# A merge that alternates computed and loaded gates, two attention blocks turned ahead, and pools of slots opened anew for each stage

## The chip, the cores and the metric

One core of one Trainium2 chip. The metric is device time in microseconds (us) of one execution of the whole program; the engines are TensorE (PE in the profile, its weight loads PEld), VectorE (DVE), ScalarE (ACT), GpSimd (POOL) and SyncE (SP), beside 16 DMA engines. SP and ACT issue the DMAs, each into its own queue.

## The reference

Two layers over 1024 latent tokens and 256 context tokens (1280 in all, 10 tiles of 128) of width 1024. Layer 1 needs no context output, so it has 8 tiles of queries where layer 0 has 10.

```python
p = modulated(x) @ w_in                      # all branches, their SiLU gates, 4 x 1024 merge gates
u0, u1, u2, u3 = neighbourhood, latent, RG-LRU, grouped-query branch of p   # each [tokens, 256]
m = sum(sigmoid(gate_i) * (u_i @ w_branch[i]) for i in range(4))            # [tokens, 1024]
x = layer_norm(alpha * x + g * (m @ w_out))  # g from the modulation vector
```

All matmuls that matter are taken in three products of a number split in a high and a low part (hi·hi, lo·hi, hi·lo), so each logical product of 128 rows is three matmul instructions.

## The kernel before, in words

The program text is written in stages, and a scheduler orders the instructions of each engine from it; each engine then works through its own list in order. Storage comes from pools: `sl` gives slots of [128, 1280] floats (13 of them, for K and V, softmax rows, accumulators, branch inputs, output rows), `wp` gives pairs of split weights `whi`/`wlo` of 512 columns (10 of them, with 2 raw buffers `wraw`), `tp` the short-lived tiles (`tmp`, `ph`, `pl`, `q`), and PSUM gives two banks each for `mm` and `t` and a wide one. A tile that takes a buffer waits for the last use of the tile that had it. Both pools live for the whole program.

One layer (function `layer`) runs so:

- `g_proj`, then `m_proj` and `a_proj` woven with the LRU branch. `put_t` (line 320 on) turns projected rows, splits them into `ph`/`pl` tiles and stores them to DRAM from ACT's queue; K, V and q are loaded from there later. The first loads of attention (K, V and q of the first head, `first_loads`) stand between `m_proj` and `a_proj`.
- Attention: 12 heads (4 grouped-query, 4 latent, 4 neighbourhood), each in units of 2 or 3 query tiles: 2, 3, 3, 2 in layer 0 and 3, 3, 2 in layer 1. `attend` makes the scores of one unit; `values` turns softmax blocks (transposes on PE, a split into `ph`/`pl` by ACT and DVE) and multiplies them with V, and is pumped between later scores. It turns one block ahead of the one it multiplies. SP loads q for the next unit (`fetch`, into a ring of three q tiles) and, at the first unit of a head, K and V of the next head (`ahead_kv`). Each q comes as two halves, and the second half of the one under way stands behind K and V in SP's queue.
- Beside attention `gates()` computes merge gates (24 matmuls for 128 output columns and 512 tokens) and stores them: all eight chunks c of the last two branches in `M_ORDER` = (2, 3, 1, 0).
- `merge()` goes over branches 2, 3, 1. Branches 2 and 3 compute their gates (24 matmuls and 6 for the branch, per chunk and group of tokens), branch 1 loads them (6 matmuls); the sigmoid is ACT's, the product DVE's, the addition to `acc` POOL's for loaded gates and else DVE's.
- `last` (line 1005 on) does branch 0 with loaded gates, splits each finished `acc` into `xh`/`xl` (40 pieces over both layers), and loads w_out.
- `outp` (line 1039 on) multiplies with w_out tile by tile, adds the residual, normalises, and in layer 0 stores `x1` and turns the result back for layer 1.

Of the kernel before, what the change touches and what calls it, by code (L numbers as in the profile page):

```python
# [16 lines left out]
D = 1024  # L17
# [19 lines left out]
G_PRE = 2  # L37
W_A = 30
W_B = 26
UNITS = [(2, 3), (5, 3), (8, 2)]  # L40
NBIAS = (E_N + M_N) * 64
# [5 lines left out]
def hybrid_kernel(ctx: ExitStack, tc, a):  # L47
# [8 lines left out]
    sm = ctx.enter_context(tc.tile_pool(name="sm", bufs=6))  # L56
    lc = ctx.enter_context(tc.tile_pool(name="lc", bufs=2))
    dr = ctx.enter_context(tc.tile_pool(name="dr", bufs=2, space=DRAM))
    ps_mm = ctx.enter_context(tc.tile_pool(name="ps_mm", bufs=2, space=PSUM))
# [57 lines left out]
    def spare():  # L117

        turns[0] += 1
        tag = ("tmp", "ph", "tmp", "pl", "tmp", "ph", "pl")[turns[0] % 7]  # L120
        return tp.tile([128, 512], F32, tag=tag, name=nm("spare"), bufs=3 if tag == "tmp" else 2)
# [5 lines left out]
    def slot(dt=F32, w=NT, s="sl"):  # L127
        return sl.tile([128, w], dt, tag="sl", name=nm(s))
# [65 lines left out]
    def row_stats(src):  # L194
        st = sm.tile([128, 2, 6], F32, tag="bnst", name=nm("bnst"))
# [36 lines left out]
    def split_w(raw, shape):  # L232
# [3 lines left out]
        hi = wp.tile([128, 512], F32R, tag="whi", name=nm("whi"))  # L236
        lo = wp.tile([128, 512], F32R, tag="wlo", name=nm("wlo"))
# [7 lines left out]
    def load_w(src, shape):  # L245
        n = 1
        for d in shape[1:]:
            n *= d
        raw = wp.tile([128, 512], F32, tag="wraw", name=nm("wraw"), bufs=2)
# [4 lines left out]
        return split_w(raw, shape)  # L254
# [37 lines left out]
    def layer(l, xh, xl, need_ctx, gate, finish, side, side2, ahead=None):  # L292
# [24 lines left out]
        gate_d = {i: dram([KC, 128, NT], F32, f"gates{i}") for i in M_ORDER[4 - G_PRE:]}  # L317
        u_d = [dram([2, 128, NT], F32, f"u{i}") for i in range(4)]

        def put_t(dst, t, first, src, rows=128):  # L320
# [6 lines left out]
            hi = tp.tile([128, 4, 128], F32R, tag="ph", name=nm("th"), bufs=2)  # L327
# [8 lines left out]
        def put_v(dst, t, src3):  # L336

            n = src3.shape[1]
            vt = tp.tile([128, 4, 128], F32R, tag="ph", name=nm("vt"), bufs=2)
# [112 lines left out]
        def lru_steps():  # L452
# [24 lines left out]
            for c in range(2):  # L477
# [20 lines left out]
                raw = wp.tile([128, 512], F32, tag="wraw", name=nm("wraw"), bufs=2)  # L498
# [67 lines left out]
        def attend(h, unit, qs, y, rcp, scores, vt):  # L566
# [7 lines left out]
            queue.append([values(64 * (h % 2), y, qts, blocks, pts, vt), len(blocks) + 1])  # L574

        def values(o, y, qts, blocks, pts, vt):
# [5 lines left out]
            def turn(vb, q0, cols):  # L582
# [4 lines left out]
                ph = tp.tile([128, 512], F32R, tag="ph", name=nm("ph"), bufs=2)  # L587
# [8 lines left out]
            st = None  # L596
            for i, b in enumerate(blocks):
                nx = turn(*b)
# [5 lines left out]
            product(nb - 1, *st)  # L604
# [83 lines left out]
        def m_load():  # L688
# [14 lines left out]
            for src, n in ((a["mla_w_uq"][l, 0:128], 384), (a["mla_w_uq"][l, 128:256], 384), (a["mla_w_ukv"][l], 512)):  # L703
                raw = wp.tile([128, 512], F32, tag="wraw", name=nm("wraw"), bufs=2)
# [11 lines left out]
        def m_steps():  # L716
# [25 lines left out]
            def second(t, has_q, y, kr):  # L742
# [4 lines left out]
                ch = tp.tile([128, 512], F32R, tag="ph", name=nm("ch"), bufs=2)  # L747
# [138 lines left out]
        def attention(jobs):  # L886
# [37 lines left out]
        def gates():  # L924

            for i in M_ORDER[4 - G_PRE:]:
                for c in range(KC):
                    w = load_chunk(w_in, C_GATE + i * D + c * 128)
                    for g in qgroups:
                        gs = slice(g[0], g[0] + g[1])  # L930
                        ps = mm()
                        xs = xs_g(g)
                        for k in range(0, KC, 2):
                            mm_b(ps[:, :g[1]], w[k:k + 2], lambda j: xs(k + j), k == 0, k == KC - 2)
                            if k < KC - 2:
                                yield
                        s = tmp()
                        act.copy(s[:, :g[1]], ps[:, :g[1]])
                        act.dma_start(gate_d[i][c, :, gs], s[:, :g[1]])
                        yield  # L940

        jobs = [make(h) for make in (g_job, m_job, a_job) for h in range(4)]
        att = attention(jobs)
        run(f"g_proj{l}", g_steps())

        def first_loads():
            next(att)
            yield

        weave(("", chain((f"m_proj{l}", m_steps()), (f"g_att{l}", first_loads()), (f"a_proj{l}", a_steps())), W_A),  # L950
              (f"lru{l}", lru_steps(), W_B))
        ticks = sum(len(qts) + len(blocks) for job in jobs for qts, blocks in job[3])
        fill.update(gen=gates(), rate=4 * KC * G_PRE * len(qgroups) / ticks, due=0.0)
# [22 lines left out]
        def merge():  # L976
            for bi, i in enumerate(M_ORDER[:3]):
                uh, ul = load_u(i)
                for c in range(KC):
                    w = None if i in gate_d else load_chunk(w_in, C_GATE + i * D + c * 128)  # L980
# [3 lines left out]
                    for g in qgroups:  # L984
                        gs = slice(g[0], g[0] + g[1])
                        sgm = tmp()
                        if w is None:
                            pm = sgm
                            sp.dma_start(sgm[:, :g[1]], gate_d[i][c, :, gs])
# [13 lines left out]
        weave((f"merge{l}", merge(), 72), (f"mod{l}", side, 50))  # L1003
# [6 lines left out]
        i = M_ORDER[3]  # L1010
        uh, ul = load_u(i)
        wb = [load_rows2(a["w_branch"][l, i], h * 512) for h in range(2)]
        for _ in fill["gen"]:
            pass
# [218 lines left out]
```

## Time and profile before

| | us |
|---|---|
| median of 3 runs (lowest, highest) | 3144.45 (3127.67, 3151.09) |
| profiled execution, its own time | 3149.83 |
| span of the profiled execution | 3148.0 |

In layer 0 attention lies at 445 to 1160 us, merge at 1163 to about 1566, `last` and `outp` up to 1768; in layer 1 the same stages begin at 2105, 2725 and 3005. PEclk is the granted TensorE clock, 1.00 being 2.4 GHz and 0.50 being 1.2 GHz, as a mean over a stretch. A DMA row in the chain of waits lasts from the point where only it is waited for to its landing; SPq is SP's own time to issue.

### The profile page before, as it was taken

To read this page: it belongs to the slowest core of one execution; us is meant where nothing else is said; L and a number is where in the kernel's file an instruction comes from. 1 tells how busy PE (TensorE), PEld (TensorE's weight loads), DVE (VectorE), ACT (ScalarE), POOL (GpSimd) and SP (SyncE) were. 2 spreads that over 40 slices of the span, in tenths; PEclk is the share of its full clock that TensorE was granted. 3 is DMA by queue.
4 is the path that set the end of the run, shared out by engine and by line. 5 is a ranking of instruction groups with operands and counts; after the bars stand their busy time and mean duration, and the time that the engine had idled before them with its cause. 6 is when DMAs were issued, how large, how long until landed. Compare 5 with 4: busy or idle time off the path is not lost.

```text
span 3148.0 us, 39813 instructions
## 1 busy us (share of the span) xinstructions
PE 2837.8 (90%) x14458; PEld 2292.2 (73%) x14458; DVE 1554.1 (49%) x3147; ACT 1270.7 (40%) x2698; POOL 235.2 (7%) x327
## 2 busy tenths in 40 slices
PE   7987979998988999999789897998999897999878
PEld 3766868787877787776457685877887786788657
DVE  5653365554545551222368644366654464523366
ACT  4353364544444451111233435265544454512230
POOL 1210000000000000000342110000000000000141
PEclk9998989998999999999799999998999998999999
DMA  7232422222323222322462323322332233212252
GB/s 256 86 106 88 118 66 65 83 89 67 92 85 97 92 94 65 71 60 90 157 173 78 119 75 115 112 83 72 89 94 75 84 102 96 78 47 64 89 159 77
DMA packets 308782, 299.83 MB, mean 95 GB/s; under 512 B 24553, under 2 KB 245993, under 8 KB 308585
## 3 DMA queue, kind: packets, MB, share of 16 engines
q1 hardware_dynamic: 177384, 202.49, 21.3%
q10 hardware_dynamic: 131200, 94.79, 9.8%
q8 instruction: 114, 1.87, 0.3%
q14 instruction: 84, 0.68, 0.1%
HBM read 217.11 MB, written 80.10 MB: 94 GB/s over the span
## 4 chain that ended last, share of the span: by engine, by line
PE 65%; DMA 15%; DVE 7%; ACT 4%; POOL 3%; issue 3%; SPq 2%; ACTq 1%; POOLq 0%; DVEq 0%
PE wide L639 5%; PE merge__mm L284 4%; PE merge__mm L285 4%; PE merge__mm L286 4%; PE wide L284 2%; PE wide L285 2%; PE wide L286 2%; PE m_att__t L586 2%; PE a_att__mm L284 2%; PE a_att__mm L285 2%; PE a_att__mm L286 2%; DMA g_att__q<-start__qkg 2%; PE g_att__t L586 2%; PE m_att__mm L286 2%; PE m_att__mm L284 2%
## 5 line engine op out<-in xcount | busy, mean ns | idle before, releaser
L284 PE MATMUL merge__mm<-xh,merge__whi 128*128 128x512 f32 (+1 forms) x640 | 240.5, 376 | 1.2 <-DVE a_att__tmp L439 1.2
L285 PE MATMUL merge__mm<-xl,merge__whi 128*128 128x512 f32 (+1 forms) x640 | 236.7, 370 | 0.0
L286 PE MATMUL merge__mm<-xh,merge__wlo 128*128 128x512 f32 (+1 forms) x640 | 236.6, 370 | 0.0
L290 DVE TENSOR_TENSOR m_att__pl<-m_att__t,m_att__ph 128x384 fp32r<-128x384 f32 (+1 forms) x248 | 121.5, 507 | 141.3 <-ACT m_att__ph L289 138.2
L289 ACT CAST m_att__ph<-m_att__t 128x384 fp32r<-128x384 f32 (+1 forms) x248 | 105.7, 441 | 148.1 <-PE m_att__t L586 101.0
L238 ACT CAST merge__whi<-merge__wraw 128x512 fp32r<-128x512 f32 (+1 forms) x112 | 59.3, 530 | 236.0 <-PE merge__mm L285 179.3
L284 PEld LDWEIGHTS merge__mm<-xh,merge__whi 128*128 128x128 f32 x640 | 121.1, 189 | 41.5 <-issue 16.5
L239 DVE TENSOR_TENSOR merge__wlo<-merge__wraw,merge__whi 128x512 fp32r<-128x512 f32 (+1 forms) x112 | 64.5, 576 | 166.2 <-ACT merge__whi L238 158.4
L290 DVE TENSOR_TENSOR g_att__pl<-g_att__t,g_att__ph 128x384 fp32r<-128x384 f32 (+1 forms) x228 | 112.8, 514 | 68.0 <-ACT g_att__ph L289 64.6
L999 DVE TENSOR_TENSOR merge__tmp<-wide,merge__tmp 128x512 f32<-128x512 f32 (+1 forms) x80 | 50.9, 637 | 176.2 <-PE wide L286 168.3
L639 PE MATMUL wide<-g_att__ks,g_att__q 128*128 128x512 f32 (+1 forms) x400 | 112.4, 380 | 26.6 <-DMA g_att__q<-start__qkg 14.0
L286 PEld LDWEIGHTS merge__mm<-xh,merge__wlo 128*128 128x128 f32 x640 | 121.3, 189 | 20.7
L289 ACT CAST g_att__ph<-g_att__t 128x384 fp32r<-128x384 f32 (+1 forms) x228 | 99.6, 446 | 89.5 <-PE g_att__t L586 80.4
L285 PEld LDWEIGHTS merge__mm<-xl,merge__whi 128*128 128x128 f32 x640 | 121.2, 189 | 19.1
L284 PE MATMUL wide<-merge__uh,merge__whi 128*128 128x512 f32 (+1 forms) x240 | 100.5, 419 | 36.9 <-DVE merge__tmp L999 26.4
L284 PE MATMUL a_att__mm<-xh,a_att__whi 128*128 128x512 f32 (+1 forms) x320 | 126.2, 395 | 0.3 <-DVE a_att__tmp L439 0.3
L993 ACT ACTIVATE merge__tmp<-merge__mm 128x512 f32<-128x512 f32 (+1 forms) x80 | 44.2, 553 | 199.6 <-PE merge__mm L286 198.4
L593 PE MATMUL m_att__pv<-m_att__ph,m_att__vs 128*128 128x384 f32 (+1 forms) x228 | 88.8, 389 | 37.3 <-ACT m_att__ph L289 37.2
L285 PE MATMUL a_att__mm<-xl,a_att__whi 128*128 128x512 f32 (+1 forms) x320 | 121.9, 381 | 0.0
L641 DVE TENSOR_SCALAR_CACHE_REDUCE m_att__p<-wide 128x1280 f32<-128x1280 f32 (+1 forms) x72 | 98.7, 1371 | 46.1 <-PE wide L639 43.1
L286 PE MATMUL a_att__mm<-xh,a_att__wlo 128*128 128x512 f32 (+1 forms) x320 | 121.1, 380 | 0.0
L639 PE MATMUL wide<-m_att__ks,m_att__q 128*128 128x512 f32 (+1 forms) x400 | 120.8, 372 | 0.4 <-DVE m_att__p L641 0.4
(415 smaller groups left out, 8060.7 us busy)
## 6 DMA issues: line engine op xcount, KB each, us to landing
merge__wraw<-in_w_in_dram SPq DMA_DIRECT2D x64, 256.0 KB
mod__wm<-in_w_mod_dram SPq DMA_DIRECT2D x48, 256.0 KB
g_proj__wm<-in_w_mod_dram SPq DMA_DIRECT2D x16, 512.0 KB
a_att__wraw<-in_w_in_dram ACTq DMA_DIRECT2D x32, 256.0 KB
last__wraw<-in_w_out_dram SPq DMA_DIRECT2D x32, 256.0 KB
g_att__wraw<-in_w_in_dram ACTq DMA_DIRECT2D x28, 256.0 KB
m_att__wraw<-in_w_in_dram ACTq DMA_DIRECT2D x28, 256.0 KB
merge__wraw<-in_w_branch_dram SPq DMA_DIRECT2D x48, 128.0 KB
```

Of the source, the lines that this page charges most:

```text
L238: act.copy(hi[:, :n], raw[:, :n])
L239: dve.tensor_sub(lo[:, :n], raw[:, :n], hi[:, :n])
L284: pe.matmul(ps, wh, xh, start=first and k == 0, stop=False)
L285: pe.matmul(ps, wh, xl, start=False, stop=False)
L286: pe.matmul(ps, wl, xh, start=False, stop=last and k == nk - 1)
L289: act.copy(hi, src)
L290: dve.tensor_sub(lo, src, hi)
L586: pe.transpose(tb[:, i * 128:(i + 1) * 128], pts[q0 + i][:, col:col + 128], ident)
L593: pe.matmul(pv[:, qr], vt[:, vb, :], ph, start=i == 0, stop=False)
L639: pe.matmul(wide[:, c0:c0 + w], qs[:, j, qi * 128:(qi + 1) * 128], k[:, c0:c0 + w], start=j == 0, stop=j == len(ks) - 1)
L641: dve.tensor_scalar(pt[:, :nk], wide[:, :nk], -scale, None, ALU.mult, ALU.min, accum_out=nb)
L999: dve.tensor_mul(sgm[:, :g[1]], pb[:, :g[1]], sgm[:, :g[1]])
```

## The change

Every odd chunk c of every branch now has its gate computed beside attention and loaded in the merge; every even one is computed in the merge. The merge goes over all four branches, and `last` keeps only the loads of w_out and the split of `acc`, in pieces of 256 columns. `outp` takes four tiles first. `values` turns two blocks ahead, with three `ph` buffers. `cut_memory` closes and reopens both pools: before `g_proj` 13 slots and 10 pairs, and after the projections 16 slots and 6 pairs. The first K, V and q loads stand behind that second opening, and `ahead_kv` is called at the second unit of a head. The last gate modulation moves from `last` into the merge. The small pools shrink.

```diff
+AHEAD = 2
...
-    wp = ctx.enter_context(tc.tile_pool(name="wp", bufs=10))
-    sl = ctx.enter_context(tc.tile_pool(name="sl", bufs=13))
...
+    def cut_memory(name, slots, pairs):
+
+        pools.close()
+        cut["sl"] = pools.enter_context(tc.tile_pool(name=f"sl_{name}", bufs=slots))
+        cut["wp"] = pools.enter_context(tc.tile_pool(name=f"wp_{name}", bufs=pairs))
...
+        gate_d = {(i, c): dram([128, NT], F32, f"gates{i}{c}") for i in M_ORDER for c in range(1, KC, 2)}
...
-                ph = tp.tile([128, 512], F32R, tag="ph", name=nm("ph"), bufs=2)
+                ph = tp.tile([128, 512], F32R, tag="ph", name=nm("ph"), bufs=3)
...
+                turned.append(turn(*b))
                 tick()
-                if st:
-                    product(i - 1, *st)
-                st = nx
+                if len(turned) > AHEAD:
+                    product(i - AHEAD, *turned.pop(0))
                 yield
...
                 if i == 0:
+                    head = begin(kv[label, h])
+                if i == 1:
                     j = jobs.index(job) + 1
                     if j < len(jobs):
                         ahead_kv(j)
-                    head = begin(kv[label, h])
...
+        cut_memory(f"a{l}", 13, 10)
         run(f"g_proj{l}", g_steps())
-
-        def first_loads():
-            next(att)
-            yield
-
...
+        weave(("", chain((f"m_proj{l}", m_steps()), (f"a_proj{l}", a_steps())), W_A), (f"lru{l}", lru_steps(), W_B))
+        cut_memory(f"b{l}", 16, 6)
+        phase[0] = f"g_att{l}"
+        next(att)
...
-            for bi, i in enumerate(M_ORDER[:3]):
+            for bi, i in enumerate(M_ORDER):
...
-                    w = None if i in gate_d else load_chunk(w_in, C_GATE + i * D + c * 128)
+                    w = None if (i, c) in gate_d else load_chunk(w_in, C_GATE + i * D + c * 128)
...
-        weave((f"merge{l}", merge(), 72), (f"mod{l}", side, 50))
+        for _ in fill["gen"]:
+            pass
+        weave((f"merge{l}", merge(), 4 * KC * len(qgroups)), (f"mod{l}", side, 68))
...
-                hi_lo(xh[:, c, gs], xl[:, c, gs], acc[c][:, gs])
...
+        wo = [[load_w(a["w_out"][l, k * 128:(k + 1) * 128, h * 512:h * 512 + 512], [128, 512], h > 0 or 2 <= k < 6)
+               for k in range(KC)] for h in range(2)]
+        for g in qgroups:
+            for c0 in range(g[0], g[0] + g[1], 256):
+                for c in range(KC):
+                    hi_lo(xh[:, c, c0:c0 + 256], xl[:, c, c0:c0 + 256], acc[c][:, c0:c0 + 256])
...
+        batches = [range(q0t, q0t + 4)] + [range(t, t + 1) for t in range(q0t + 4, TT - 2)]
```

What this moves, at three places. First ACT, layer 0, in the third branch of the merge (L993 before and L1005 after is the sigmoid; a source `mm` is a gate computed just now, a source `tmp` a loaded one; L238 and L249 split a weight). Before:

```order
1370 L993 ACTIVATE merge__tmp_13143<-merge__tmp_13143 128x256
1371 L993 ACTIVATE merge__tmp_13154<-merge__tmp_13154 128x512
1372 L993 ACTIVATE merge__tmp_13168<-merge__tmp_13168 128x512
1373 L993 ACTIVATE merge__tmp_13188<-merge__tmp_13188 128x256
1374 L238 CAST last__whi_13567<-last__wraw_13565 128x512
1375 L993 ACTIVATE merge__tmp_13199<-merge__tmp_13199 128x512
```

After the change, in the third branch too:

```order
1313 L1005 ACTIVATE merge__tmp_12028<-merge__mm_12029 128x512
1314 L249 CAST merge__whi_12287<-merge__wraw_12285 128x512
1315 L1005 ACTIVATE merge__tmp_12072<-merge__tmp_12072 128x256
1316 L1005 ACTIVATE merge__tmp_12083<-merge__tmp_12083 128x512
1317 L1005 ACTIVATE merge__tmp_12097<-merge__tmp_12097 128x512
1318 L249 CAST merge__whi_12293<-merge__wraw_12291 128x512
1319 L1005 ACTIVATE merge__tmp_12129<-merge__mm_12130 128x256
```

Where loaded chunks followed one another, three loaded groups now lie between groups of computed ones.

Second SP, layer 0, where the first K (`ks`) and V (`vs`) of attention are loaded. Before, amid the weights of `a_proj`:

```order
72 L253 DMA a_proj__wraw_2869<-in_w_in_dram 128x256
73 L660 DMA g_att__ks_2340<-start__qkg_108 128x1x1280
74 L665 DMA g_att__vs_2342<-start__vg_111 128x10x128
75 L253 DMA a_proj__wraw_2875<-in_w_in_dram 128x256
76 L253 DMA a_proj__wraw_2881<-in_w_in_dram 128x256
```

After:

```order
86 L264 DMA lru__wraw_3422<-in_w_in_dram 128x4x128
87 L664 DMA g_att__q_3531<-start__qkg_102 128x1x384 x2
88 L664 DMA g_att__q_3548<-start__qkg_102 128x1x384 x2
89 L465 DMA lru__lrucols_15894<-in_lru_cols_dram 128x22
90 L673 DMA g_att__ks_3524<-start__qkg_102 128x1x1280
91 L678 DMA g_att__vs_3526<-start__vg_105 128x10x128
92 L664 DMA g_att__q_3628<-start__qkg_102 128x1x256 x2
```

They have moved behind the last weights of the projections; the table `lrucols` of layer 1 stands before them, and the slot that K takes is one of the newly opened pool.

Third SP, layer 0, the next pair of K and V inside attention, with the q tile that they divide. Before:

```order
95 L651 DMA g_att__q_4101<-start__qkg_108 128x1x384
96 L660 DMA g_att__ks_3963<-start__qkg_108 128x1x1280
97 L665 DMA g_att__vs_3965<-start__vg_111 128x10x128
98 L651 DMA g_att__q_4101<-start__qkg_108 128x1x384
99 L651 DMA g_att__q_4168<-start__qkg_108 128x1x256 x2
```

After:

```order
95 L664 DMA g_att__q_4119<-start__qkg_102 128x1x384 x2
96 L664 DMA g_att__q_4190<-start__qkg_102 128x1x256
97 L673 DMA g_att__ks_4122<-start__qkg_102 128x1x1280
98 L678 DMA g_att__vs_4124<-start__vg_105 128x10x128
99 L664 DMA g_att__q_4190<-start__qkg_102 128x1x256
```

K and V divide the q of the fourth unit of a head (256 columns) where they divided that of the third (384 columns).

## Rows read from the trace of the kernel before

**Rows 1.** The page: span, busy time of the engines, granted clock, chain that ended last.

```profile
span 3148.0 us, 39813 instructions
...
PE 2837.8 (90%) x14458; PEld 2292.2 (73%) x14458; DVE 1554.1 (49%) x3147; ACT 1270.7 (40%) x2698; POOL 235.2 (7%) x327
...
PE 65%; DMA 15%; DVE 7%; ACT 4%; POOL 3%; issue 3%; SPq 2%; ACTq 1%; POOLq 0%; DVEq 0%
```

**Rows 2.** Windows by stretch: start:end, length, busy time of each engine, then PEclk.

```profile
225.00:300.00 75.00, 50.99 (x209) 39.67 (x210) 31.66 (x51) 30.91 (x57) 0.00 (x0) 0.80 0.32 95
375.00:450.00 75.00, 53.63 (x261) 43.37 (x260) 43.84 (x55) 43.65 (x60) 0.00 (x0) 0.84 0.24 68
450.00:1150.00 700.00, 653.04 (x3772) 557.23 (x3771) 381.15 (x873) 354.52 (x795) 10.92 (x32) 0.96 0.27 83
...
1300.00:1350.00 50.00, 43.44 (x202) 33.35 (x202) 13.43 (x24) 10.93 (x23) 0.00 (x0) 0.90 0.36 69
...
1475.00:1650.00 175.00, 140.38 (x535) 86.19 (x535) 83.76 (x130) 58.43 (x111) 61.20 (x52) 0.82 0.58 172
1725.00:1775.00 50.00, 40.24 (x198) 32.65 (x196) 33.33 (x62) 31.12 (x71) 6.44 (x12) 0.87 0.40 127
1900.00:2000.00 100.00, 75.55 (x358) 60.01 (x357) 46.03 (x90) 45.29 (x97) 3.34 (x6) 0.88 0.36 109
2100.00:2150.00 50.00, 35.84 (x183) 28.87 (x181) 27.84 (x47) 24.52 (x45) 0.00 (x0) 0.88 0.35 101
2150.00:2725.00 575.00, 539.96 (x2947) 450.59 (x2946) 325.34 (x719) 298.25 (x658) 9.19 (x27) 0.96 0.28 84
2750.00:2950.00 200.00, 200.00 (x884) 165.62 (x883) 56.52 (x92) 41.76 (x79) 0.00 (x0) 1.00 0.20 52
2950.00:3075.00 125.00, 92.89 (x338) 63.72 (x338) 73.06 (x97) 44.13 (x76) 47.31 (x34) 0.93 0.48 150
```

**Rows 3.** Groups of 1475 to 1650 us: busy, mean ns, idle before, releaser.

```profile
L1027 POOL TENSOR_TENSOR merge__acc<-merge__acc,last__spare 128x512 f32<-128x512 f32 (+1 forms) x24 | 30.5, 1288 | 28.7 <-DVE last__spare L1026 28.7
L284 PE MATMUL wide<-merge__uh,merge__whi 128*128 128x512 f32 (+1 forms) x50 | 26.1, 522 | 13.6 <-DVE merge__tmp L999 13.6
L290 DVE TENSOR_TENSOR xl<-merge__acc,xh 128x512 fp32r<-128x512 f32 (+1 forms) x24 | 18.6, 781 | 10.8 <-ACT xh L289 10.4
```

**Rows 4.** Chain of waits in the projections of layer 0: start, length, what.

```profile
258.42 8.11 DMA start__qkm<-m_proj__th
...
267.06 9.06 DMA start__qkm<-m_proj__th
```

**Rows 5.** Chain of waits at the end of the LRU branch, layer 0.

```profile
423.04 12.03 DMA lru__lrucols<-in_lru_cols_dram
```

**Rows 6.** SP's timeline around the second K and V of layer 0.

```profile
468.51 0.48 SPq L660 DMA_DIRECT2D g_att__ks<-start__qkg  x1
469.09 3.54 SPq L665 DMA_DIRECT2D g_att__vs<-start__vg  x1
472.68 26.87 SPq L651 DMA_DIRECT2D g_att__q<-start__qkg  x5
```

**Rows 7.** Chain of waits in the attention of layer 0.

```profile
472.68 23.21 DMA g_att__q<-start__qkg
...
721.77 15.28 SPq L653
737.10 11.42 DMA m_att__q<-start__qkm
```

**Rows 8.** Windows of 25 or 50 us in attention: PE busy, PEclk.

```profile
2400.00:2450.00 50.00, 41.03 (x198) 0.92 0.29 88
...
725.00:775.00 50.00, 39.47 (x211) 0.83 0.19 63
...
2650.00:2675.00 25.00, 13.31 (x55) 0.73 0.32 96
```

More of the change, by code (lines that the diff above doesn't have):

```diff
@@ L120, in spare @@
         tag = ("tmp", "ph", "tmp", "pl", "tmp", "ph", "pl")[turns[0] % 7]
-        return tp.tile([128, 512], F32, tag=tag, name=nm("spare"), bufs=3 if tag == "tmp" else 2)
+        return tp.tile([128, 512], F32, tag=tag, name=nm("spare"), bufs=2 if tag == "pl" else 3)
     def bank():
@@ L230, in xm_tile, with split_w @@
             hi_lo(xh[:, 4 * h:4 * h + 4, ts], xl[:, 4 * h:4 * h + 4, ts], v3)
-    def split_w(raw, shape):
+    def split_w(raw, shape, far=False):
         n = 1
@@ L235, in split_w @@
             n *= d
-        hi = wp.tile([128, 512], F32R, tag="whi", name=nm("whi"))
-        lo = wp.tile([128, 512], F32R, tag="wlo", name=nm("wlo"))
+        if far:
+            both = slot(F32R, w=1024, s="wboth")
+            hi, lo = both[:, :512], both[:, 512:]
+        else:
+            hi = cut["wp"].tile([128, 512], F32R, tag="whi", name=nm("whi"))
+            lo = cut["wp"].tile([128, 512], F32R, tag="wlo", name=nm("wlo"))
         act.copy(hi[:, :n], raw[:, :n])
@@ L243, in split_w, with load_w @@
         return hi[:, :n], lo[:, :n]
-    def load_w(src, shape):
+    def load_w(src, shape, far=False):
         n = 1
@@ L253, in load_w @@
         wq[0].dma_start(dst, src)
-        return split_w(raw, shape)
+        return split_w(raw, shape, far)
     def load_rows(w2, c0, n):
@@ L290, in hi_lo, with layer @@
         dve.tensor_sub(lo, src, hi)
-    def layer(l, xh, xl, need_ctx, gate, finish, side, side2, ahead=None):
+    def layer(l, xh, xl, need_ctx, gate, finish, side, ahead=None):
         w_in = a["w_in"][l]
@@ L573, in attend @@
                 pump(len(qts) - qi)
-            queue.append([values(64 * (h % 2), y, qts, blocks, pts, vt), len(blocks) + 1])
+            queue.append([values(64 * (h % 2), y, qts, blocks, pts, vt), len(blocks) + AHEAD])
         def values(o, y, qts, blocks, pts, vt):
@@ L1045, in layer @@
                 bcast(ts[h], a[src][l, h * 512:(h + 1) * 512], 512)
-        gt, pairs = None, []
-        for t in range(q0t, TT):
-            if gt is None or t == CT:
-                gt = [tp.tile([128, 512], F32, tag="q", name=nm("gt"), bufs=3) for _ in range(2)]
-                for h in range(2):
-                    bcast(gt[h], gd[1 if t < CT else 0, h * 512:(h + 1) * 512], 512)
-            pairs.append((t, slot(w=D, s="Y")))
-            if need_ctx and t == TT - 2:
-                continue
+        gt = {}
+        batches = [range(q0t, q0t + 4)] + [range(t, t + 1) for t in range(q0t + 4, TT - 2)]
+        batches += [range(TT - 2, TT)] if need_ctx else [range(t, t + 1) for t in range(TT - 2, TT)]
+        for batch in batches:
+            pairs = [(t, slot(w=D, s="Y")) for t in batch]
             for h in range(2):
@@ L1057, in layer @@
                 for t, Y in pairs:
+                    s = 1 if t < CT else 0
+                    if s not in gt:
+                        gt[s] = tp.tile([128, 1024], F32, tag="q", name=nm("gt"), bufs=3)
+                        bcast(gt[s], gd[s], 1024)
                     ps = bank()
@@ L1072, in layer @@
                 finish(t, Y, later)
-            pairs = []
         while later:
@@ L1123, in start @@
         yield from xm_group(CT + 4, 4)
+    ctx.push(pools)
     x1 = dr.tile([SEQ, D], F32, name="x1", bufs=1)
@@ L1132, in later_mods @@
         yield from modulation(1, 0, 2048, mc1, raw_w, 512)
+        yield from modulation(1, 2048, 1024, gate1, raw_w, 512)
     def fin0(t, Y, later):
@@ L1143, in hybrid_kernel @@
     fin0.x_rows = rows0
-    layer(0, xh, xl, True, gate0, fin0, later_mods(), modulation(1, 2048, 1024, gate1, raw_w, 512), start())
+    layer(0, xh, xl, True, gate0, fin0, later_mods(), start())
     def fin1(t, Y, later):
```

100 lines of the change are left out of this document (36 added, 64 removed).

## The prediction

> **What bounds the kernel now.** I read the page first, then windows of 25 us of TensorE with its granted clock, then the stretches where something is lost, then the chain of waits inside them. TensorE is busy for 2837.8 of 3148.0 us and holds 65% of the chain, DMAs 15%, VectorE 7% [rows 1]. So time is to be had only where TensorE waits, or where after a wait its clock stands at the lower of its two levels. I measure both by one number: the length of a stretch less (busy time x granted clock). In a stretch without loss, 2750 to 2950 us, the busy time is 200.00 at 1.00 with 884 recorded matmuls, nearly all of 512 columns, which is 0.226 us each [rows 2]. By that measure the losses are:
>
> - the end of the merge: 175 - 140.38 x 0.82 = 59.9 us in layer 0, 125 - 92.89 x 0.93 = 38.6 in layer 1, and 50 - 43.44 x 0.90 = 10.9 at 1300 to 1350, where the inputs of the next branch are loaded;
> - attention: 700 - 653.04 x 0.96 = 73.1 in layer 0, 575 - 539.96 x 0.96 = 56.6 in layer 1;
> - the middle of the projections: 75 - 50.99 x 0.80 = 34.2 and 100 - 75.55 x 0.88 = 33.5;
> - the end of the LRU branch: 75 - 53.63 x 0.84 = 30.0 and 50 - 35.84 x 0.88 = 18.5;
> - the passage from layer 0 to layer 1: 50 - 40.24 x 0.87 = 15.0 [rows 2].
>
> These make some 370 us. The change touches every one of them, with both signs.
>
> **The merge, -85 us.** Where a loaded chunk follows a loaded chunk, a group of 512 tokens has 6 matmuls, 6 x 0.226 = 1.4 us of TensorE, and one POOL addition of 1.29 us, a split piece of 0.78 us on VectorE and the loads; the branch's matmuls wait for VectorE's product (13.6 us before L284) [rows 3], and 52 POOL instructions make 61.20 us of POOL in that stretch [rows 2]. Alternated, a computed chunk (30 matmuls per group) puts 6.8 us of TensorE beside each loaded group, so POOL, VectorE and the loads have five times the cover. The number of computed and loaded chunks is the same as before; only their order differs. I take the 59.9 + 38.6 + 10.9 = 109.4 us as gone; the 10.9 go because 16 slots less 8 accumulators less 4 branch inputs leave 4 free for the next inputs. Given back: the split of `acc` stands alone at the end now, and `outp` needs its first 256 columns, 8 pieces of about 0.39 us (half of 0.781 us) [rows 3], 3 us on VectorE, beside ACT's part and the last addition, say 5. Seven to eight of the sixteen w_out blocks can be loaded only into slots that `acc` leaves, while the first batch covers 4 tiles x 24 matmuls x 0.226 = 22 us; in layer 0 the 40 pieces take 40 x 0.39 = 16 us before the last slot is free, so part of the loads shows, say 7. That makes 12 us a layer, and -109 + 24 = -85. Bounds: -109 (nothing shows) and -45 (the cover is hit as badly as half of the loss now).
>
> **Attention, -23 us.** K and V of a head take long: K is issued at 468.51, and the half q behind V, on which the chain then rests for 23.21 us from 472.68, lands at 495.9, so the two and that half take 27.4 us [rows 6, 7]. The same is seen at 721.77, where SP sits 15.28 us in one issue and the q then takes 11.42 more [rows 7]; TensorE loses 50 - 39.47 x 0.83 = 17.2 us there [rows 8]. What decides is how much work lies between the release of that q's buffer (three tiles in the ring, so three units earlier) and its use. In layer 0, with units of 2, 3, 3, 2 query tiles, the q divided before is that of the third unit: units one and two cover, 5 tiles. After, it is that of the fourth: units two and three, 6 tiles. A tile is 700 / 120 = 5.8 us. A stall of about ten us so loses some 6 of it, and I take half of 73.1, -36. In layer 1 the units are 3, 3, 2: before, units one and two covered, 6 tiles; now the q divided is the next head's first, and units two and three cover, 5 tiles, 6.0 us less. Four stalls there grow by about 6 us each, +24; of the 15.3 us (25 - 13.31 x 0.73) at 2650 [rows 8], where weights of the merge were in the queue, I count 6 as gone: +18 together. Turning two blocks ahead: `pl` and the PSUM tile for turns still have two buffers, so a third block can't be far along; -5. Sum -36 + 18 - 5 = -23. Bounds: -100 (no q is ever late, because K and V no longer wait for slots at all) and +40 (layer 0 gains nothing, layer 1 loses at every head).
>
> The Trainium skill (DMA: Bandwidth & Descriptors, section Bandwidth) gives 6.15 us for a load of 1 MB. By it K and V of 0.64 MB each would be, as an estimate from that page, about 8 us, no q would be late at any place in the queue, and the moves of K and V would be worth nothing. The trace disagrees: 27.4 us, with V's rows of 512 bytes in it [rows 6, 7].
>
> **Projections, -34 us.** Two stores of `m_proj` rows hold the chain for 8.11 and 9.06 us [rows 4]; the first K and V, now issued after the projections, were in the DMA queues just then, and the three `ph` buffers let a turn go on while one store is late. Those two pieces are half of 34.2, so I take half of 34.2 + 33.5. Bounds: 0 (the stores are slow by themselves) and -55.
>
> **The second opening of the pools, +32 us.** Every first user of a new slot waits for the last users of the old pool: K waits for the LRU's last store (u2) and V comes behind it. What was loaded a hundred us early now starts at the end of the LRU branch, 27.4 us to the landing of V by [rows 6, 7] and some 5 for the store (no row; 0 to 10). TensorE has two gate products of 24 matmuls and some 24 of the first scores, 72 x 0.226 = 16 us, before its list comes to the first product with V. So about 16 us open in each layer, with the slow clock behind them 22. In layer 0 the wait of 12.03 us for `lrucols` goes [rows 5], since it no longer stands where the LRU's next step waits on that queue. 2 x 22 - 12 = +32. Bounds: -12 (all covered) and +80.
>
> **The first opening in layer 1, +18 us.** Layer 1's first weights and tables now need the old pool empty, so the stores of `x1` and the last norms; 8 loads of 256 KB at the 172 GB/s of the merge's end [rows 2] are 12 us, and 6 for the latency of the stores. The matmuls of layer 1 that stood between the last turns of layer 0 go behind them. Bounds: 0 and +40.
>
> The smaller pools of statistics and the moved modulation I cost at nothing: their work is hidden beside TensorE's in the merge, where VectorE is busy for 56.52 of 200 us [rows 2].
>
> **Sum.** -85 - 23 - 34 + 32 + 18 = -92. Against the profiled execution, 3149.83, that is 3058; the median of the runs, 3144.45, lies 5 lower, so 3053, and I say 3055. All bounds on the good side give -109 - 100 - 55 - 12 + 0 = -276, all on the bad side -45 + 40 + 0 + 80 + 40 = +115.
>
> **Rivals.** (a) With 16 slots K and V leave early enough, and no q is late: -85 - 100 - 34 + 32 + 18 = -169, about 2975. For it: more slots. Against: the releases that count are those of the ring of q, which the change leaves alone. (b) The merge gives only half, since w_out, 6 pairs of weights and the split become a stall of their own at the end, and the projections give 15: -45 - 23 - 15 + 32 + 18 = -33, about 3113. For it: 40 pieces on two engines and sixteen loads must pass before `outp` is through its first batch. (c) The slower side: the pools' openings are full stops. Each of the three empties TensorE's list until stores have landed and the first weights or K and V are there; at 27.4 us for K and V, 10 for the store, nothing to cover, and the lower clock afterwards, one costs some 60 us, three 180: -85 - 23 - 34 + 180 = +38, about 3185. It decides from 47 us each on. Against it: gate weights come from another pool and give 48 matmuls. (d) K and V land almost at once when nothing else is in the queue, so that their place there is worth nothing: attention gives only the -5, the second opening only -12: -85 - 5 - 34 - 12 + 18 = -118, about 3027. Against it: 27.4 us [rows 6, 7]. The Trainium skill's figure named above would have it so.
>
> **Chances.** Forecast 0.48 (its own range 3005 to 3105), (a) 0.18, (b) 0.17, (c) 0.13, (d) 0.04. A measurement of this kernel tells about 1%, 31 us, from no change, so faster means under 3113. The forecast is almost all faster, (a) and (d) too, (b) about a third: 0.74. Same 0.13, slower 0.13. For 8 in 10 the range reaches to most of (a) and past (b): 2955 to 3145.
>
> **What would show it.** Right: no stretch of the merge under 22 us of 25 before its last 20 us, with POOL's additions spread evenly; a gap of 15 to 30 us at the end of each LRU branch, ending with a DMA of u2, `ks` or `vs`; fewer and shorter q waits in layer 0's attention and longer ones in layer 1's; no `lrucols` in the chain; a gap with x1's stores before layer 1's first matmuls. Wrong: a merge whose second half still runs under 20 us of 25; a gap over 47 us at an opening; layer 1's attention shorter than 575 us by more than 20 us.

## The result and the profile after

The changed kernel takes 3105.98 us (median of 5 runs, 3102.01 to 3110.97) against 3139.2 us for the kernel before (5 runs, 3127.67 to 3151.09): a ratio of 0.990, 95% interval 0.9866 to 0.9934. It is faster by 33 us (1.0%), where 92 us were forecast against the profiled execution; the time lies in the stated range of 2955 to 3145, but the gain is little over a third of the one forecast. Of the difference of 59 us, 11 us are the profiled execution of before itself, 3149.83 us, which lay that far over the median of the five runs; the other 48 are looked for below by comparing the two profiled executions, 3149.83 and 3105.85 us.

The page of the changed kernel, with the lines of [rows 1]:

```profile
span 3104.0 us, 40366 instructions
...
PE 2820.9 (91%) x14458; PEld 2271.1 (73%) x14458; DVE 1558.1 (50%) x3207; ACT 1269.2 (41%) x2738; POOL 205.9 (7%) x307
...
PE 70%; DMA 12%; DVE 5%; ACT 4%; issue 2%; POOL 2%; SPq 1%; ACTq 1%; POOLq 0%; DVEq 0%
```

DMAs still hold 12% of the chain, where they held 15%. The windows by stretch answer to [rows 2] (same columns; the stretches follow the stages, which now lie elsewhere):

```profile
225.00:300.00 75.00, 58.10 (x253) 44.56 (x252) 32.00 (x51) 32.87 (x60) 0.00 (x0) 0.89 0.31 92
375.00:475.00 100.00, 46.22 (x194) 35.92 (x193) 41.64 (x69) 39.25 (x52) 0.00 (x0) 0.68 0.19 55
475.00:1150.00 675.00, 644.19 (x3763) 547.42 (x3763) 378.65 (x847) 350.54 (x792) 10.64 (x32) 0.98 0.27 85
1250.00:1325.00 75.00, 67.89 (x324) 50.50 (x323) 22.35 (x40) 17.84 (x37) 5.55 (x5) 0.95 0.43 108
1550.00:1650.00 100.00, 84.34 (x360) 64.54 (x359) 62.66 (x120) 29.38 (x66) 15.37 (x19) 0.93 0.34 95
1700.00:1750.00 50.00, 31.73 (x136) 24.39 (x135) 24.78 (x43) 26.24 (x58) 5.24 (x9) 0.73 0.27 91
1875.00:1975.00 100.00, 82.10 (x379) 65.60 (x378) 48.15 (x101) 49.10 (x108) 3.25 (x9) 0.88 0.34 100
2075.00:2125.00 50.00, 27.26 (x95) 20.44 (x94) 20.91 (x23) 15.09 (x19) 0.00 (x0) 0.71 0.37 103
...
2925.00:3050.00 125.00, 120.88 (x501) 93.76 (x500) 76.39 (x129) 39.55 (x84) 19.61 (x16) 0.99 0.37 117
```

By the same measure (length less busy time x clock) the end of the merge in layer 1 now loses 125 - 120.88 x 0.99 = 5 us where it lost 38.6, and in layer 0 100 - 84.34 x 0.93 = 22 where it lost 59.9. The stretch of layer 0 in which the inputs of the next branch are loaded still loses 75 - 67.89 x 0.95 = 10.5 us, where it lost 10.9. TensorE's longest wait in it is the same, first before the change (1310 to 1360 us), then after it (1240 to 1340):

```profile
PE wide L284 <- ACT merge__uh L289: 6.6, 1, 6.6
```

```profile
PE wide L295 <- ACT merge__uh L300: 6.4, 1, 6.4
```

So is the load that the chain of waits rests on there, before and after:

```profile
1318.83 10.17 DMA merge__tmp<-start__u
```

```profile
1270.10 9.47 DMA merge__tmp<-start__u
```

And 375 to 475 us, the opening of attention in layer 0, loses 100 - 46.22 x 0.68 = 69 us, where 375 to 450 lost 30.0 (and the same 100 us 31); layer 1's opening loses 31 us for 18.5, and the passage between the layers 50 - 31.73 x 0.73 = 27 for 15.0. The chain of waits in layer 0's opening shows what the 69 are:

```profile
421.56 13.22 DMA lru__lrucols<-in_lru_cols_dram
...
443.18 3.37 DMA start__u<-lru__lruo
446.63 15.39 DMA g_att__ks<-start__qkg
```

The wait for the table [rows 5] is still there, 13.22 us. Then the store of u2, and only after it K, on which all scores wait for 15.39 us. TensorE's waits in 395 to 475 us say the same in one row (waiting line, what for, us in total, times, longest):

```profile
PE wide L652 <- DMA g_att__ks<-start__qkg: 43.0, 1, 43.0
```

And in layer 1, in 2040 to 2130 us:

```profile
PE wide L652 <- DMA g_att__ks<-outp__qkg: 16.5, 1, 16.5
```

To see where time went I cut each execution at the same instructions: the last LRU matmul, the first score of attention, the first matmul of the merge, the last normalisation of the output stage, and the last `g_proj` matmul of layer 1. Lengths in us, worked out from the first and last starts in the tile views of each profiled execution (experiments, below, in the same table):

| stage | before | after | e3 | e4 | e5 | e7 | e9 | e10 |
|---|---|---|---|---|---|---|---|---|
| start to last LRU matmul, layer 0 | 401.4 | 394.2 | 390.9 | 399.1 | 400.1 | 399.3 | 387.4 | 396.1 |
| to the first score | 17.1 | 68.2 | 11.2 | 15.7 | 15.7 | 15.7 | 51.3 | 11.3 |
| to the first merge matmul | 744.7 | 705.3 | 731.2 | 731.3 | 739.7 | 741.1 | 727.0 | 729.8 |
| merge and output stage, layer 0 | 597.2 | 555.8 | 556.6 | 559.3 | 558.7 | 560.5 | 556.5 | 545.8 |
| to the last `g_proj` matmul, layer 1 | 60.6 | 81.4 | 78.5 | 62.2 | 61.1 | 61.3 | 61.3 | 78.4 |
| to the last LRU matmul | 264.5 | 264.3 | 270.0 | 278.9 | 265.3 | 274.1 | 259.2 | 269.3 |
| to the first score | 2.5 | 44.8 | 1.6 | 2.6 | 2.6 | 2.6 | 38.6 | 1.5 |
| to the first merge matmul | 651.1 | 607.5 | 633.9 | 642.3 | 637.7 | 632.0 | 628.1 | 626.3 |
| merge and output stage, layer 1 | 405.0 | 378.7 | 374.1 | 380.7 | 375.6 | 376.0 | 375.7 | 376.3 |

The merge and output stages give 41.4 + 26.3 = 67.7 us. The first scores come 51.1 and 42.3 us later after the LRU branch than before, of which the rest of attention gives back 39.4 and 43.6. The passage costs 20.8.

### The profile page after: what moved, and what is told of

The parts are those of the page before. It is cut to its first block, busy times and chain, and to the rows that moved or that the text cites. A ratio compares the mean times of both kernels' runs of the same rounds, so it can differ in the third digit from the quotient of the medians.

```text
span 3104.0 us, 40366 instructions
## 1 busy us (share of the span) xinstructions
PE 2820.9 (91%) x14458; PEld 2271.1 (73%) x14458; DVE 1558.1 (50%) x3207; ACT 1269.2 (41%) x2738; POOL 205.9 (7%) x307
## 4 chain that ended last, share of the span: by engine, by line
PE 70%; DMA 12%; DVE 5%; ACT 4%; issue 2%; POOL 2%; SPq 1%; ACTq 1%; POOLq 0%; DVEq 0%
PE wide L652 6%; PE merge__mm L295 4%; PE merge__mm L296 4%; PE merge__mm L297 4%; PE wide L295 3%; PE wide L296 3%; PE wide L297 3%; PE m_att__t L597 2%; PE a_att__mm L295 2%; PE a_att__mm L296 2%; PE a_att__mm L297 2%; PE m_att__mm L297 2%; PE m_att__mm L296 2%; PE m_att__mm L295 2%; PE g_att__t L597 2%
## 5 line engine op out<-in xcount | busy, mean ns | idle before, releaser
L249 ACT CAST merge__whi<-merge__wraw 128x256 fp32r<-128x256 f32 (+1 forms) x128 | 65.7, 513 | 253.9 <-PE merge__mm L296 175.5
L1011 DVE TENSOR_TENSOR merge__tmp<-wide,merge__tmp 128x512 f32<-128x512 f32 (+1 forms) x120 | 76.5, 638 | 175.9 <-PE wide L297 160.2
L250 DVE TENSOR_TENSOR merge__wlo<-merge__wraw,merge__whi 128x256 fp32r<-128x256 f32 (+1 forms) x128 | 72.1, 563 | 141.0 <-ACT merge__whi L249 132.7
L295 PE MATMUL wide<-merge__uh,merge__whi 128*128 128x256 f32 (+1 forms) x320 | 126.5, 395 | 15.4 <-ACT merge__uh L300 10.6
L654 DVE TENSOR_SCALAR_CACHE_REDUCE g_att__p<-wide 128x1280 f32<-128x1280 f32 (+1 forms) x72 | 98.5, 1369 | 71.0 <-PE wide L652 70.8
L652 PEld LDWEIGHTS wide<-g_att__ks,g_att__q 128*128 128x128 f32 x400 | 73.7, 197 | 80.2 <-issue 60.3
L1012 POOL TENSOR_TENSOR merge__acc<-merge__acc,merge__tmp 128x512 f32<-128x512 f32 (+1 forms) x60 | 78.3, 1305 | 635.2 <-DVE merge__tmp L1011 635.2
L654 DVE TENSOR_SCALAR_CACHE_REDUCE m_att__p<-wide 128x1280 f32<-128x1280 f32 (+1 forms) x72 | 98.7, 1371 | 41.8 <-PE wide L652 41.4
```

The costliest lines, as they stand in the source:

```text
L249: act.copy(hi[:, :n], raw[:, :n])
L250: dve.tensor_sub(lo[:, :n], raw[:, :n], hi[:, :n])
L295: pe.matmul(ps, wh, xh, start=first and k == 0, stop=False)
L652: pe.matmul(wide[:, c0:c0 + w], qs[:, j, qi * 128:(qi + 1) * 128], k[:, c0:c0 + w], start=j == 0, stop=j == len(ks) - 1)
L654: dve.tensor_scalar(pt[:, :nk], wide[:, :nk], -scale, None, ALU.mult, ALU.min, accum_out=nb)
L1011: dve.tensor_mul(sgm[:, :g[1]], pb[:, :g[1]], sgm[:, :g[1]])
```

## The experiments

The times of e1 to e4 come from one chip, those of e5 to e8 from a second and those of e9 to e11 from a third; on these the kernel before took 3136 to 3145 us. Within such a group times compare directly; across groups, and with the changed kernel, ratios to the kernel before do (0.001 is 3 us). The stages come from one profiled execution of each kernel, and executions of one kernel differ by up to 13 us in the experiments (e4), so that a stage's difference of a few us shows little by itself.

**The table `lrucols` (e1).**

```diff
-            cols = lc.tile([128, 22], F32, tag="lrucols", name=nm("lrucols"), bufs=1)
+            cols = lc.tile([128, 22], F32, tag="lrucols", name=nm("lrucols"), bufs=2)
```

> The changed kernel with two buffers for the table lrucols (and a 64-byte constant put elsewhere to make room), so that layer 1's load of it no longer waits for layer 0's last use. Theory A (VectorE's list holds layer 1's constants ahead of the last steps of layer 0's LRU, so the 13.22 us wait for that table delays the whole opening of attention in layer 0): the wait goes, the first scores move from 462 to about 450 us, and the kernel takes 10 to 13 us less than the changed one, some 3094 us. Theory B (the store of u2 and the load of K would have held TensorE as long anyway): under 3 us less.

3100.28 us, ratio 0.9862 (0.9839 to 0.9885), against 0.990: 6 us less by the medians, 12 by the ratios, with intervals that touch, so the time alone does not settle it. The trace does: the table is now loaded at the start, K is issued at 435.45 us instead of 446.63, and the first score comes 10.6 us sooner (451.8 against 462.4). Theory A. That the wait stayed in the changed kernel lies in the order that the scheduler made: VectorE's list has layer 1's first constant (line 469), which reads that table, before the last steps of layer 0's LRU.

**Early K and V (e2), and both (e3).**

```diff
-            t = slot(F32R, s="ks")
+            t = keep_tile("kk", F32R) if own else slot(F32R, s="ks")
...
-        cut_memory(f"a{l}", 13, 10)
+        cut_memory(f"a{l}", 11, 10)
...
-        cut_memory(f"b{l}", 16, 6)
-        phase[0] = f"g_att{l}"
-        next(att)
+        cut_memory(f"b{l}", 14, 6)
```

with V done likewise, `first_loads` between `m_proj` and `a_proj` again, and the two tiles lent to the first two output rows later.

> The changed kernel with the first K and V in two tiles of their own, loaded between m_proj and a_proj as before the change (11 and 14 slots in the pools, so the memory is the same). Theory A (the opening costs what K takes to land behind the barrier of the pools, 15.39 and 17.92 us): both waits go, the kernel takes 25 to 38 us less than the changed one, some 3074 us, and the projections stay as they are. Theory B (K and V beside the stores of m_proj bring back the two stalls of 8 and 9 us in each layer): the projections get 15 to 25 us longer over both layers, and the kernel takes 0 to 15 us less, some 3098 us.

> Both edits together. Theory A: the two gains add, 35 to 50 us less than the changed kernel, some 3063 us, and TensorE has no dead stretch of over 15 us at the ends of the LRU branches. Theory B (one hides the other, since the table's wait runs beside nothing but K's): no more than the better of the two alone.

e2: 3057.8 us, ratio 0.9723 (0.9701 to 0.9746), 48 us under the changed kernel by the medians and 56 by the ratios. e3: 3050.87 us, ratio 0.9705 (0.9681 to 0.9728), 55 us under it by the medians. The dead stretch is gone (in e3 11.2 and 1.6 us to the first score), and the projections stayed as they were within 6 us in each layer. Both are theory A, with more than it said: it had counted the landings of K, 15.39 and 17.92 us, where TensorE waited 43.0 and 16.5. On top of e2, on the same chip, the second buffer is worth 7 us, and by itself 6 or 12, so the two gains add, as far as the times can tell.

**Pools opened once (e4).**

```diff
-        cut_memory(f"a{l}", 13, 10)
...
-        cut_memory(f"b{l}", 16, 6)
-        phase[0] = f"g_att{l}"
-        next(att)
...
-               ... [128, 512], h > 0 or 2 <= k < 6)
+               ... [128, 512], h > 0)
...
+    cut_memory("all", 13, 10)
```

> The changed kernel with its pools opened once, 13 slots and 10 pairs for the whole program, first loads between m_proj and a_proj as before, and the first eight blocks of w_out in pairs. Theory A (the openings lose more than 16 slots give): the 44 and 42 us by which the first scores come late, and the 19 us between the layers, go, the attention keeps most of its gain, and the kernel takes 30 to 60 us less than the changed one, some 3060 us. Theory B (the 16 slots are what shortened the waits for q in attention): attention grows by 30 to 45 us over both layers, and the kernel is within 15 us of the changed one.

3072.77 us, ratio 0.9763 (0.9736 to 0.979): 33 us less than the changed kernel by the medians and 43 by the ratios, theory A. Without the openings the passage is 62.2 us instead of 81.4. With 13 slots attention keeps the greater part of its gain (731.3 + 15.7 = 747.0 us from the last LRU matmul to the merge, 761.8 before; 644.9 in layer 1, 653.6 before).

**The merge alone (e5).** e4 with `AHEAD = 1`, two `ph` buffers and `ahead_kv` at the first unit.

> The kernel with its pools opened once, and of the change only the merge, the end of it and the first batch of four tiles in the output stage: one block turned ahead, two ph buffers, K and V of the next head asked for at the first unit. Theory A (the merge is worth what its two stages show, 40 and 27 us by the profile of the changed kernel): 60 to 70 us less than the kernel before, some 3080 us, and attention as long as before. Theory B (the other parts of the change carry a good part of the 72 us that the kernel with pools opened once gains): under 50 us less, over 3095 us.

3066.42 us, ratio 0.9783 (0.9768 to 0.9798): 70 us less than before on the same chip, theory A. The merge and output stages give 38.5 + 29.4 us, as in the changed kernel. By the profiles attention is shorter too, by 6.4 and 13.3 us; a part of that may be the profiled execution of before, which lay 11 us over the median; the rest is open. So the merge, with its end and the first batch, carries the gain of 2.2%; against e4 (0.9763) nothing else of the change shows a gain beyond the intervals.

**One block ahead (e6), K and V at the first unit (e7).**

```diff
-AHEAD = 2
+AHEAD = 1
```

> Pools opened once, and one block turned ahead in place of two. Theory A (pl and the PSUM tile for turns have two buffers, so the second block ahead gives little): within 6 us of the kernel with pools opened once, 3067 to 3079 us. Theory B (two blocks ahead cover the two handings over between engines): 10 to 25 us more, 3083 to 3098 us, spread evenly over both attentions.

3074.31 us, ratio 0.9808 (0.9791 to 0.9825), against 0.9763 (0.9736 to 0.979). By the medians theory A, by the ratios 14 us more: unclear between the two. In the traces the stretch from the last LRU matmul to the merge is 750.8 us against 747.0 in layer 0, and 647.2 against 644.9 in layer 1: 6 us, near the 5 that the prediction had, but too little for single executions to show. Against e5, on the same chip, e6 is 8 us slower, and their runs don't overlap (3062 to 3070 and 3071 to 3081); e6 has besides three `ph` buffers and asks for K and V at the second unit.

```diff
-                if i == 1:
+                if i == 0:
                     j = jobs.index(job) + 1
                     if j < len(jobs):
                         ahead_kv(j)
```

> Pools opened once, and K and V of the next head asked for at the first unit of a head, as before the change. Theory A (the cover of the divided q counts, 5 query tiles against 6): the attention of layer 0 gets 20 to 36 us longer and that of layer 1 15 to 24 us shorter, the whole some 3080 us. Theory B (what counts is the load itself, wherever it stands): both attentions within 8 us, the whole within 8 us of 3073.

3071.81 us, ratio 0.9795 (0.9777 to 0.9813). The same stretch is 756.8 against 747.0 us in layer 0, 9.8 longer, and 634.6 against 644.9 in layer 1, 10.3 shorter: the two signs of theory A, at half of the low end of its sizes in layer 0 and two thirds of it in layer 1, and a time that is within theory B's. In layer 0 the other kernels bear the sign out: 745.1 to 750.8 us with the second unit (e4, e6, e11), 755.4 to 761.8 with the first (before, e5, e7). In layer 1 they don't: 644.9 and 647.2 us with the second unit (e4, e6), and 634.6 to 653.6 with the first (before, e5, e7, e11, the last with 650.9).

**The second half of w_out later (e8).** e3 with

```diff
-        wo = [[load_w(...) for k in range(KC)] for h in range(2)]
+        wo = [load_wo(0)]
...
+                if h == len(wo):
+                    wo.append(load_wo(h))
```

in the loop over the halves, before the first four tiles.

> The changed kernel with early K and V and the second buffer for lrucols, and the loads of the second half of w_out asked for after the first four tiles have had the first half. Theory A (those loads, 4.77, 9.70 and 10.97 us in the chain, hold ACT's and VectorE's lists, and behind them the products that free PSUM): the wait of 14.29 us of TensorE at the start of the output stage in layer 0 goes, and the kernel takes 8 to 20 us less than without this edit (3051), some 3037 us. Theory B (TensorE then waits for the same weights a little later): within 5 us of 3051.

3041.96 us, ratio 0.9704 (0.9689 to 0.972), where e3 had 0.9705: no difference by the ratios, 9 us by the medians on two chips, so the time alone does not settle it. The stage does: merge and output of layer 0 take 546.2 us, 10.4 less than in e3. The chain of the changed kernel shows the wait that it removes:

```profile
1574.36 4.77 DMA last__wraw<-in_w_out_dram
...
1580.52 9.70 DMA last__wraw<-in_w_out_dram
...
1591.62 10.97 DMA last__wraw<-in_w_out_dram
```

Each is one block of 256 KB, followed by ACT's cast and VectorE's subtraction; VectorE's list has these subtractions before the products that free PSUM. TensorE's waits in 1570 to 1630 us of the changed kernel, in 1535 to 1600 of e3, and there in e8:

```profile
PE wide L287 <- DVE outp__Y L1054: 14.5, 2, 14.3
```

```profile
PE wide L290 <- DVE outp__kv L1060: 10.3, 2, 10.1
```

```profile
PE wide L290 <- DVE outp__kv L1065: 0.8, 1, 0.8
```

**K and V late without a reopening (e9).** e5 with one edit:

```diff
-        def first_loads():
-            next(att)
-            yield
...
+        phase[0] = f"g_att{l}"
+        next(att)
```

after the projections.

> The kernel with the merge alone and pools opened once (3066 us), with one edit: the first K, V and q of attention are asked for after the projections, as in the changed kernel, but with no reopening of pools. Theory A (what the openings cost is the barrier: K can't take a slot until the LRU's last store has landed): K finds a slot early, the first scores come within 10 us of where they were, TensorE's waits for the tl tiles of m_proj fall from 18 and 16 us to 6 as in the changed kernel, and the whole is 5 to 20 us less, some 3055 us. Theory B (the late place in SP's queue is enough): the first scores come 15 us or more later in each layer, and the whole is 10 to 40 us more, some 3090 us.

3093.66 us, ratio 0.9842 (0.9812 to 0.9871) against 0.9783 for e5: 18 us more by the ratios, theory B. Here no pool is reopened, and SP issues K at 414.33 us, before the LRU branch is through; TensorE still waits

```profile
PE wide L652 <- DMA g_att__ks<-start__qkg: 31.3, 1, 31.3
```

and the first scores come 35.6 and 36.0 us later than in e5. So the late place in SP's queue alone does most of the harm. In layer 0 a q load stands in front of K in that queue, and SP itself waits there for a matmul of the LRU branch (380 to 480 us):

```profile
SPq L664 <- PE wide L297: 31.7, 1, 31.7
```

In the changed kernel the first scores come 16.9 us (68.2 - 51.3) later still in layer 0 and 6.2 in layer 1. That is what the barrier of the pools can add, though the two kernels differ in slots, `ph` buffers and blocks ahead as well. The other half of the forecast shows too: TensorE's longest wait for the `tl` tiles of `m_proj` falls, from before (215 to 300 us)

```profile
PE m_proj__t L326 <- DVE m_proj__tl L290: 11.9, 2, 10.0
PE m_proj__t L746 <- DVE m_proj__tl L290: 5.4, 2, 5.2
```

to, in e9 (200 to 300 us),

```profile
PE m_proj__t L337 <- DVE m_proj__tl L301: 3.7, 2, 2.8
PE a_proj__t L337 <- DVE m_proj__tl L301: 2.6, 1, 2.6
```

and the projections get 12.7 us shorter in layer 0 and 6.1 in layer 1.

**All mends (e10), and with pools opened once (e11).** e10 is e8 with

```diff
-                if i == 0:
-                    head = begin(kv[label, h])
-                if i == 1:
+                if i == (1 if need_ctx else 0):
```

and `begin` behind it; e11 is e5 with the same line, the second buffer for `lrucols` and w_out later.

> The changed kernel with all mends that were found: early K and V in tiles of their own, a second buffer for lrucols, the second half of w_out later, and K and V of the next head asked for at the second unit in layer 0 and at the first in layer 1. Theory A (the cover of the divided q, 6 query tiles in both layers): 5 to 12 us less than without the last edit (3042), some 3034 us. Theory B (in this kernel other waits take its place): within 4 us of 3042.

> The kernel with the merge alone and pools opened once (3066 us), one block turned ahead, with the three other mends: a second buffer for lrucols, the second half of w_out later, and K and V of the next head asked for at the second unit in layer 0 and at the first in layer 1. Theory A (each is worth here what it was worth there: 6 to 10, 8, and 7 to 10 us): some 3042 us, so the openings of the pools and the second block ahead are of no use at all. Theory B (16 slots and two blocks ahead carry part of the 3042 us): 3050 us or more.

e10: 3040.14 us, ratio 0.9667 (0.964 to 0.9694), the best of all, 66 us under the changed kernel; against e8 it is 2 us less by the medians (theory B) and 12 by the ratios (theory A), so the last edit is not settled. Its layer 1 has 626.3 us from the first score to the merge where e8 has 633.5, and TensorE loses little at the end of layer 0's merge:

```profile
1525.00:1625.00 100.00, 94.01 (x400) 70.84 (x400) 66.86 (x133) 37.48 (x85) 14.56 (x21) 0.98 0.34 96
```

e11: 3051.14 us, ratio 0.9705 (0.9679 to 0.9732), theory B. On the same chip every run of e10 (3035 to 3042 us) lies under every run of e11 (3049 to 3054), so what e10 has besides is worth some 11 us together: the openings with 14 slots, K and V in tiles of their own, two blocks ahead, three `ph` buffers. Which of these it is was not tried.

## Why the prediction was wrong

The sum was -92; stage by stage the profiled executions give -44. The signs of all terms held. The step that failed most is that on the projections, 27 us of the 48; two items of the merge term in layer 0 make 18 more.

- **Projections, -34: measured -7.** The two long waits went as said, in layer 0 from 11.9 and 5.4 to a few us. But the stretch 225 to 300 still loses 75 - 58.10 x 0.89 = 23 us, in many waits of 1 to 3 us between ACT, VectorE and TensorE, and in layer 1 1875 to 1975 loses 100 - 82.10 x 0.88 = 28, where 33.5 were lost. The step took the two stores' 17 us as a saving because they made half of the loss; what stood behind them was not asked. e9 puts the move of K and V alone at 12.7 + 6.1 us. Why the changed kernel keeps 7 of these 19 is open. The third `ph` buffer is a suspect: with K and V early, layer 1's projections take 274.1 to 278.9 us in the three kernels that have it (e4, e6, e7), and 265.3 and 263.7 in the two that have two (e5, e11). Layer 0 does not show it, and it was not tried by itself.
- **The merge, -85: measured -68.** The mechanism of alternating held, and e5 shows it without the other parts. In layer 0 two items of the term were mis-sized, 41.4 us for 59. The 10.9 us at the inputs of the next branch did not go: 10.5 are left. The step saw free slots there, but the loads waited for go through the short-lived `tmp` tiles, whose three buffers the change leaves alone; that they are what holds the loads was not tried. And the end of the merge loses 22 us, where 12 were given back. The prediction had priced the exposed w_out loads at 7 us, as transfers; they cost as waits at the head of ACT's and VectorE's lists, 14.3 us of TensorE, and e8 gives 10.4 us back in that stage. Layer 1 comes out at 26.3 us for 38.6 - 12 = 26.6, with some luck: the end of its merge gained 33, and what took 7 of it back was not looked for.
- **The second opening, +32: measured some +48.** From the last LRU matmul to the merge the changed kernel takes 773.5 and 652.3 us, e3 742.4 and 635.5: 31.1 + 16.8 = 47.9. (e3 lacks the wait for the table too, and its first score comes after 11.2 us where it came after 17.1 before; so some 6 us of this cost, and of the gain of attention below, may be the table's.) Three things in the step were wrong. It counted 24 scores as cover, and no score can run without K, which alone took 15.39 and 17.92 us; it let the 12 us of `lrucols` go, which stayed at 13.22; and it blamed the barrier, where e9 shows that the late place is enough. The store of u2 was sized well (5 us; 3.37 in the chain). The 6 us for the slow clock came from no row; in layer 0 the clock stood at 0.50 from the first score at 462.4 to 470 us, with TensorE busy for 6.49 us, so it cost some 3.
- **Attention, -23: measured some -37.** Taken in e3, which keeps the opening but loads K early: 761.8 to 742.4 and 653.6 to 635.5 us. Layer 0 was to give 36 and gave 19, layer 1 was to lose 18 and gained 18, and that the sum comes near is luck. What failed is the price of a late q. Of the 73.1 us lost in layer 0 before the change, TensorE's own waits for a q are 15.7 (418 to 1163 us):

```profile
PE wide L639 <- DMA g_att__q<-start__qkg: 14.0, 4, 5.9
PE wide L858 <- DMA a_att__q<-start__qka: 1.7, 1, 1.7
```

In layer 1 there are none, before or after, so the four stalls that were to grow by 6 us each were not there. The rule of the cover has its sign in layer 0 (e7, 9.8 us for the forecast 36) and is not settled in layer 1. What the rest of the gain is, which e5 has too in part, is open.

- **The passage, +18: measured +20.8**, and 62.2 us with pools opened once, about as before (60.6). The chain there holds layer 1's first table and weights (3.89, 2.73, 4.33 and 3.27 us), as forecast, and no store.

With the two errors on attention and its opening nearly cancelling (+9 forecast, +10.4 measured), the miss is the projections (27 us) and layer 0's merge (18 us), beside the 11 us of the profiled execution. Of the signs named, the gap in layer 0 (43.0 us) is over the 15 to 30 forecast, `lrucols` is in the chain, no q wait grew in layer 1, and one window of the merge has 19.43 of 25 us (1275 to 1300, the inputs).

Rival (b), a w_out stall and small gains in the projections, comes nearest to the time (3113) and named both, though its merge of -45 is under the measured -68. Rival (c) had the mechanism that costs the changed kernel most, at three openings of some 31, 17 and 21 us, well under the 47 from which it decides. Rival (a) had its premise come true, since TensorE waits for no q after the change, but the waits were 15.7 us and not 100, and with 13 slots hardly more are left (3.7 and 3.4 us in e4). Rival (d) falls with the 15 to 18 us of K, which has nothing else beside it in the DMA engines for most of them (last section).

## What to carry to other kernels

Reordering work so that a thin stage lies between thick ones was worth 2.2% here, without the other parts of the change. A scheduled load is part of the schedule: when a pool is reopened or a stage is cut, list what was loaded early across that cut and keep its tiles out of the pool. And a wait that is taken away is worth no more than what is late behind it: sum the remaining waits of the engine in that stretch before counting the gain. The same sum, of TensorE's own waits for a q, would have shown that late q's held 15.7 us in layer 0's attention, where a gain of 36 was counted.

## What the runs showed of the hardware that was not expected

A load of K, 640 KB in rows of 5 KB, took 15.39 and 17.92 us from the point where only it was waited for, with V's 640 KB issued 0.56 us behind it in layer 0:

```profile
446.63 0.50 SPq L673 DMA_DIRECT2D g_att__ks<-start__qkg  x1
447.19 0.46 SPq L678 DMA_DIRECT2D g_att__vs<-start__vg  x1
```

V is not the main reason. From 452 to 460 us the packets of K are all that moves, and they keep 12.8% of sixteen engines busy, the time of two:

```profile
DMA packets 83, 0.42 MB, mean 53 GB/s; under 512 B 0, under 2 KB 0, under 8 KB 83
...
q1 hardware_dynamic: 83, 0.42, 12.8%
```

At 53 GB/s the 640 KB take 12 us. The first K of the kernel before does the same from 262 to 266 us, with V issued only at 266.59 (34 packets, 0.17 MB, 10.8%, beside stores on the other queue). So a K takes some 12 us or more by itself in these two places, and the rows of V, which the prediction names beside its 27.4 us, are not the reason for that part. K is read as two blocks of 64 rows, the high and the low part; whether another order of its rows would put more engines to work was not tried.

A single block of w_out of 256 KB took 9.70 and 10.97 us beside the broadcasts of the gains and the residual rows, while the DMA engines were busy for 0.57 of 1575 to 1600 us.
